# Rows of a float32r matmul stream moved to a fixed place modulo 512 bytes

## The chip, the cores and the metric

The kernel runs on one core of one Trainium2 chip. The metric is the device time of one execution in microseconds, the median of three runs: 2297.84 us before the change (2295.18 to 2297.98). Profiles are of one execution each.

## What is computed

Two transformer blocks in a row on 256 tokens with 2048 features, all in float32. Cut to what matters here:

```python
SEQ, D_MODEL, D_FF = 256, 2048, 5632

def first_block(x, ...):
    h = rms_norm(x, mix_norm_g)
    q, kv, gate_logits, conv_in = split(h @ w_in)      # NSA attention and a conformer convolution
    x = x + concatenate([attn, conv]) @ w_out
    h = rms_norm(x, ffn_norm_g)
    u = causal_depthwise_conv(h @ w_up, cw, cb)        # 2048 x 11264
    a, gate = split(u)
    x = x + (silu(gate) * a) @ w_down                  # 5632 x 2048
    return rms_norm(x, final_norm_g)

def second_block(x, c, positions, ...):
    shift_m, scale_m, gate_m, shift_f, scale_f, gate_f = split(silu(c) @ w_ada + b_ada)
    h = rms_norm_2(x, g_pre_mix) * (1.0 + scale_m) + shift_m
    z = h @ w_in                                       # into MLA attention and gated linear attention
    o = concatenate([o_mla, o_gla]) @ w_out
    x = x + gate_m * rms_norm_2(o, g_post_mix)
    h = rms_norm_2(x, g_pre_ffn) * (1.0 + scale_f) + shift_f
    f = (silu(h @ w_ffn_gate) * (h @ w_ffn_up)) @ w_ffn_down
    return x + gate_f * rms_norm_2(f, g_post_ffn)
```

## The kernel before

Activations live on the chip transposed: features on the 128 partitions, the 256 tokens (`T`) on the free axis. A *row* in this text is one tile row of that kind, 128 partitions x 256 float32 values, which is 1024 bytes in each partition. `XT` holds the 16 rows of the residual stream, and `XH`, `XL` the rows that the products read.

All large products run as float32r matmuls on operands split in two. ACT copies a piece of weights, 128x1024, from its raw buffer to `wh` (`split_h`, line 454), DVE subtracts that from the raw values into `wl` (`split_l`, line 461), and the rows are split the same way into `XH` and `XL`. Three products are summed in PSUM: high x high, high x low and low x high. The weights come as a stream of pieces over SP's DMA queue into raw buffers (three of 2048 columns), three pieces ahead of their use (`LA = 3`).

`run_group` (line 549) walks through the groups of output columns in a fixed order: w_in of block 1 (to about 275 us of the span), w_out (`oh`/`ol` rows to 354, `ch`/`cl` rows of the convolution to 399), then the FFN in two halves of up-products (from the X rows) and down-products (from the `hh`/`hl` rows, called hid here: 399 to 656 up, 656 to 785 down, and again), then block 2: w_in, the MLA products, w_out (1423 to 1515) and the SwiGLU FFN with up- and down-products in turn to the end. There are two modes. In mode "w" a 128x128 slice of weights is loaded and a row of 256 columns moves; the groups `z0`, `z1`, `f0_0` and `f0_1`, first behind an adaptive norm, move 258 columns, of which the last two both carry the shift. In mode "x" a 128x128 slice of a row is loaded and 512 weight columns move (four groups of w_in and the down-products of block 2). PE meets the three products of each row in the order in which `run_group` issues them.

All other work (norms, both attentions, convolution, gated linear attention, the modulation from `w_ada`) is written as generators that a planner issues beside the products, when its own clock says that an engine has come to them (`Clock`, `Side`, `tick`). Each instruction is issued by one helper, so the profile puts all of them at line 303; the tiles' names tell them apart.

What the change touches:
- `setup` (745): the tiles `XT`, `XH` and `XL` (16 rows of T + 2 floats each, 1032 bytes apart), `vecs`, `kc`. They live for the whole kernel in the pool `cp`, which hands out addresses in the order of these calls.
- `block1_setup` (762): the tiles of block 1's mixers, among them `oh` and `ol` (8 rows each), the attention's output for w_out.
- `pre_u0_0` (1209) and `pre_f0_0` (1828): `hh` and `hl_`, 22 rows in block 1 and 16 in block 2, the hidden rows of the FFN.
- `pre_z0` (1361): `qn` and `kn`, one tile per head, whose place `mla_gen` (1606) takes over for the MLA's output rows (`oh0`..., `ol0`...).
- `xsrc` (604), `feed_shift` (647), `ev_shift` (1470) and `ev_f` (1896): which rows a product reads, how the shift is written behind the rows, and how it is read back from PSUM, into `sh`.

Of the kernel before, what the change touches and what calls it, by code (L numbers as in the profile page):

```python
"""Two transformer blocks (NSA attention + conformer conv + conv-GLU FFN, then MLA + GLA + SwiGLU
FFN with adaptive norms) on one core.

Activations live on the chip transposed: features on the partitions, the 256 tokens on the free
axis.  Weight products run as float32r matmuls: every float32 operand is split on the chip into two
float32r parts (hi + lo, 24 mantissa bits together) and hi*hi + hi*lo + lo*hi are accumulated.
"""
# [28 lines left out]
# ----------------------------------------------------------------------------- weight stream  # L36
# [4 lines left out]
def make_plan():  # L41
    """Groups of column tiles, in the order in which the tensor engine meets them."""
# [106 lines left out]
AHEAD = 2  # L149
GROUPS, MCS, TILES, WLEN = make_plan()  # L150
# [26 lines left out]
# ----------------------------------------------------------------------------- small arrays  # L177
# [103 lines left out]
# ----------------------------------------------------------------------------- the kernel  # L281
def rev(a, n):
    """a[:, n - 1 :: -1]."""
    return bass.AP(tensor=a.tensor, offset=a.offset + n - 1, ap=[list(a.ap[0]), [-1, n]])


def halves(i, n):
    """The first piece of weights is split in two steps."""
    return ((0, n // 2), (n // 2, n)) if i == 0 else ((0, n),)


class Engine:
    """Issues on an engine, and tells the clock what was issued."""
# [13 lines left out]
class Clock:  # L307
    """About when each engine comes to the end of what it was given (in us).  Work is issued in segments: a segment
    starts when its inputs are there, and the next segment of the same work when this one has ended."""
# [29 lines left out]
    def run(self, f, dep):  # L339
        """Issues a segment; its value, its end and whether it issued anything."""  # L340
        old = self.dep, self.ends, self.n
        self.dep, self.ends, self.n = dep, {}, 0
        v = f()
        end = max(self.ends.values(), default=dep) + (self.LAT if self.n else 0)
        n = self.n
        self.dep, self.ends, self.n = old
        return v, end, n


class Flags:  # L350
    """What has been issued, from the time on at which it will be done."""
# [11 lines left out]
class Side:  # L363
    """Work that runs beside the products of the weights: a generator that yields after each segment (or, with a number,
    is left alone for that many us; "dve": until DVE has little left to do)."""
# [5 lines left out]
class Kern:  # L371
# [16 lines left out]
    # ---- helpers  # L388
# [12 lines left out]
    def bank(self):  # L401
        """A PSUM bank; free() gives it back once its last reader has been emitted."""
# [8 lines left out]
    def need(self, n):  # L411
        """Waits until n banks can be had without holding up the products of the weights."""
# [31 lines left out]
    # ---- weight stream  # L444
# [28 lines left out]
    def next_mc(self, i):  # L473
        """High parts LA pieces ahead, low parts one piece less."""
# [10 lines left out]
    def tick(self):  # L485
        """Issues what is due beside the products by the time that the tensor engine gets here."""
# [20 lines left out]
    def idle(self):  # L507
        """The tensor engine has to wait: on to the next time at which something is ready."""
# [16 lines left out]
    def later(self, f, norm):  # L525
        """As soon as the products are done (and, where f needs it, the norm's factor is there)."""
# [22 lines left out]
    def run_group(self, g):  # L549
# [20 lines left out]
        for mi in g["mcs"]:  # L570
# [8 lines left out]
            for u in range(nt if g["mode"] == "w" else 2):  # L579
                o = ps[u][:min(n, 128), :N] if g["mode"] == "w" else ps[u][:, :n]  # L580
                for q, k in enumerate(m["ks"]):
# [7 lines left out]
                    for i, (a, b) in enumerate(p):  # L589
                        self.mm(o, a, b, k == 0 and i == 0, k == kl and i == 2)  # L590
# [13 lines left out]
    def xsrc(self, k, N=T):  # L604
        return self.XH[:, k, :N], self.XL[:, k, :N]

    def ready(self, key, k):
        """Row k of what the group reads has been emitted."""
# [10 lines left out]
    # ---- norms  # L619
    # The first groups after a norm run on rows without the norm's per-token factor, which their  # L620
    # evacuation applies; meanwhile the rows are rewritten with the factor for the groups after them.
# [25 lines left out]
    def feed_shift(self, b):  # L647
        """Two more columns that carry the shift."""
        bb = b[:, :, None].to_broadcast([128, 16, 2])
        self.act(self.XH[:, :, T:], bb, AF.Copy)  # L650
        self.tt(self.XL[:, :, T:], bb, self.XH[:, :, T:].bitcast(F32), OP.subtract)
# [42 lines left out]
    def warm(self):  # L694
        """Loads the table of the square root before it is waited for."""
        self.act(self.kc[:, 3:4], self.eps, AF.Sqrt)

# [3 lines left out]
    def sums(self, parts):  # L701
        """Sum over the partitions (and over parts), in every partition."""
# [10 lines left out]
    # ---- program  # L713
# [31 lines left out]
    def setup(self):  # L745
        a = self.a
        self.XT = self.cp.tile([128, 16, T], F32, name="XT")
        self.XH = self.cp.tile([128, 16, T + 2], F32R, name="XH")
        self.XL = self.cp.tile([128, 16, T + 2], F32R, name="XL")
        self.vecs = self.cp.tile([128, VEC.n], F32, name="vecs")  # L750
        self.kc = self.cp.tile([128, 4], F32, name="kc")
        self.v.memset(self.kc[:, 0:1], EPS)
# [8 lines left out]
    # ======================================================================= block 1, mixers  # L761
    def block1_setup(self):
        tc, a, ph = self.tc, self.a, self.ph
        self.p1 = ph.enter_context(ExitStack())
        P = self.b1 = self.p1.enter_context(tc.tile_pool(name="b1", bufs=1))
        self.cat = P.tile([128, CA.n], F32, name="cat")
        self.sy.dma_start(self.cat[:, :16], a["ca"][:, :16])
        self.cacc = [P.tile([128, 4, T], F32, name=f"cacc{b}") for b in range(2)]
# [8 lines left out]
        self.oh = P.tile([128, 8, T], F32R, name="oh")  # L777
        self.ol = P.tile([128, 8, T], F32R, name="ol")
# [20 lines left out]
        # keeps the tensor engine's clock up until the first rows are there  # L799
# [120 lines left out]
    def bias_gen(self):  # L920
# [23 lines left out]
        # block n of the second 128 tokens is as far away as block n - 8 of the first; from block 7 on none is complete  # L944
# [13 lines left out]
    def cmp_gen(self):  # L958
        yield
        for kv in range(2):  # L960
            self.sy.dma_start(self.w1.rearrange("p l f -> p (l f)"), self.a["w1"][kv])
            # the even places of a block in the lower half of the partitions, the odd ones in the upper half
# [86 lines left out]
    def stat_sq(self, js, src=None, scale=None, acc="ss"):  # L1049
        """Running sum of squares over tiles of XT."""  # L1050
# [45 lines left out]
    def att_gen(self, n):  # L1096
        """Head u of pair p; its keys lie in half u of the partitions."""
# [53 lines left out]
        # columns of PT: per branch [keys 0:128 x all tokens | keys 128:256 x tokens 128:256], then cmp  # L1151
# [22 lines left out]
        # the two heads side by side, in halves of the array's columns  # L1174
# [25 lines left out]
    # ======================================================================= block 1, FFN  # L1200
# [8 lines left out]
    def pre_u0_0(self):  # L1209
# [8 lines left out]
        self.hh = P.tile([128, 22, T], F32R, name="hh")  # L1218
        self.hl_ = P.tile([128, 22, T], F32R, name="hl")
# [5 lines left out]
        self.adaT = self.cp.tile([128, 96], F32, name="adaT")  # L1225
        self.cs = self.cp.tile([128, 16], F32, name="cs")
# [3 lines left out]
    def ada_gen(self, c0, c1, P, nk, bufs, every):  # L1230
        """Column groups c0 to c1 of the modulation, nk rows of tiles at a time, one such piece every so many us."""
# [10 lines left out]
        for cg in range(c0, c1):  # L1242
# [13 lines left out]
            # sums over the partitions side by side in the array's columns, then back on to the partitions  # L1256
# [757 lines left out]
```

## Time and profile before

| | before |
|---|---|
| median of three runs | 2297.84 us (2295.18 to 2297.98) |
| span of the profiled execution | 2296.4 us |
| busy PE / weight loads | 2267.4 us (99%) / 2165.5 us (94%) |
| busy DVE / ACT / POOL | 1700.1 us (74%) / 1187.9 us (52%) / 4.9 us (0%) |
| DMA | 499.22 MB, mean 217 GB/s |

The span runs from the first to the last instruction of one profiled execution on the slowest core. Busy times add up an engine's instructions; PE and its weight loads (PEld) overlap. Matmuls are pipelined, so the duration of one is longer than the distance between the starts of two, and a busy PE need not be PE at its peak.

### The profile page before, as it was taken

The numbers are of one execution on the slowest core, as the hardware profiler recorded it, in microseconds if no ns is written. First come the engines' busy times: TensorE is split into PE (matmuls) and PEld (weight loads), VectorE is DVE, ScalarE is ACT, GpSimd is POOL, SyncE is SP. The second block draws the span as 40 slices with busy tenths as digits, with TensorE's granted clock in tenths as the row PEclk, the third lists the DMA queues.
The fourth block names the chain that finished last, engine by engine and source line by source line (L and its number), as shares of the span: only waits on it lengthen the run. The fifth ranks groups of instructions, "written<-read, shape, count | busy, mean of one in ns | idle before, by whom it ended". The sixth has DMA issues, their size and how long they took to land.

```text
span 2296.4 us, 42341 instructions
## 1 busy us (share of the span) xinstructions
PE 2267.4 (99%) x17486; PEld 2165.5 (94%) x17486; DVE 1700.1 (74%) x2631; ACT 1187.9 (52%) x1826; POOL 4.9 (0%) x16
## 2 busy tenths in 40 slices
PE   8999999999999999999999999999999999999997
PEld 8998889999999999999999889989997999889986
DVE  6998888898887788888879866577666565444455
ACT  5447786655553355555556664455444444344443
POOL 0000000000000000000000000000000000000000
PEclk9999999999999999999999999999999999999999
DMA  6544325688878787877756643546666665555553
GB/s 236 181 168 156 124 80 196 230 297 290 302 280 298 283 290 286 294 276 281 256 200 221 229 139 138 196 145 207 240 235 235 244 235 189 192 182 171 184 183 129
DMA packets 89089, 499.22 MB, mean 217 GB/s; under 512 B 9904, under 2 KB 12352, under 8 KB 42432
## 3 DMA queue, kind: packets, MB, share of 16 engines
q1 hardware_dynamic: 88896, 496.51, 61.5%
q8 instruction: 137, 2.24, 0.4%
q14 instruction: 56, 0.46, 0.1%
HBM read 494.35 MB, written 2.12 MB: 216 GB/s over the span
## 4 chain that ended last, share of the span: by engine, by line
PE 93%; DVE 4%; ACT 2%; issue 1%; DMA 1%; SPq 0%; DVEq 0%; ACTq 0%
PE ps L303 93%; DVE wl L303 1%; DMA raw<-in_wst_dram 1%; DVE cacc L303 0%; ACT wh L303 0%; DVE og L303 0%; ACT P L303 0%; ACT XH L303 0%; ACT L303 0%; DVE XL L303 0%; DVE ss L303 0%; DVE blk L303 0%; ACT vt L303 0%; ACT y L303 0%; DVE XT L303 0%
## 5 line engine op out<-in xcount | busy, mean ns | idle before, releaser
L303 ACT ACTIVATE wh<-raw 128x1024 fp32r<-128x1024 f32 (+2 forms) x741 | 781.7, 1057 | 910.7 <-PE ps L303 767.6
L303 DVE TENSOR_TENSOR wl<-raw,wh 128x1024 fp32r<-128x1024 f32 (+2 forms) x741 | 899.1, 1217 | 476.5 <-PE ps L303 410.9
L303 PE MATMUL ps<-XH,wh 128*128 128x256 f32 (+1 forms) x3840 | 1096.9, 286 | 2.6 <-ACT XH L303 2.6
L303 PE MATMUL ps<-XH,wl 128*128 128x256 f32 (+1 forms) x3840 | 1085.9, 283 | 3.9 <-DVE wl L303 3.9
L303 PE MATMUL ps<-XL,wh 128*128 128x256 f32 (+1 forms) x3840 | 1083.4, 282 | 0.1
L303 PEld LDWEIGHTS ps<-XH,wh 128*128 128x128 f32 x3840 | 726.1, 189 | 10.3 <-issue 5.8
L303 PEld LDWEIGHTS ps<-XH,wl 128*128 128x128 f32 x3840 | 727.9, 190 | 4.9 <-DVE wl L303 4.9
L303 PEld LDWEIGHTS ps<-XL,wh 128*128 128x128 f32 x3840 | 729.1, 190 | 1.0 <-DVE XL L303 0.6
L303 DVE SCALAR_TENSOR_TENSOR ac<-wa,cs,ac 128x512 f32<-128x512 f32 x360 | 269.7, 749 | 6.4
L303 PE MATMUL ps<-hh,wh 128*128 128x256 f32 x704 | 200.3, 285 | 0.0
L303 PE MATMUL ps<-hh,wl 128*128 128x256 f32 x704 | 199.2, 283 | 0.0
L303 PE MATMUL ps<-hl,wh 128*128 128x256 f32 x704 | 199.2, 283 | 0.0
L303 PE MATMUL ps<-wh,hh 128*128 128x512 f32 x352 | 139.0, 395 | 0.0
L303 PE MATMUL ps<-wl,hh 128*128 128x512 f32 x352 | 138.8, 394 | 0.0
L303 PE MATMUL ps<-wh,hl 128*128 128x512 f32 x352 | 138.8, 394 | 0.0
L303 PEld LDWEIGHTS ps<-hh,wh 128*128 128x128 f32 x704 | 135.0, 192 | 1.2 <-issue 1.2
L303 PEld LDWEIGHTS ps<-hl,wh 128*128 128x128 f32 x704 | 135.1, 192 | 0.0
L303 PEld LDWEIGHTS ps<-hh,wl 128*128 128x128 f32 x704 | 135.1, 192 | 0.0
L303 DVE SCALAR_TENSOR_TENSOR cacc<-upad,cat,cacc 128x256 f32<-128x256 f32 x240 | 99.8, 480 | 0.3 <-ACT cacc L303 0.2
L303 PEld LDWEIGHTS ps<-wh,hh 128*128 128x128 f32 x352 | 65.9, 187 | 16.4 <-issue 0.2
L303 PEld LDWEIGHTS ps<-wl,hh 128*128 128x128 f32 x352 | 65.9, 187 | 16.3
L303 PEld LDWEIGHTS ps<-wh,hl 128*128 128x128 f32 x352 | 65.9, 187 | 15.9
(321 smaller groups left out, 2113.3 us busy)
## 6 DMA issues: line engine op xcount, KB each, us to landing
raw<-in_wst_dram SPq DMA_DIRECT2D x363, 1024.0 KB, 4.9
wa<-in_wada_dram SPq DMA_DIRECT2D x176, 512.0 KB, 6.0
wa<-in_wada_dram SPq DMA_DIRECT2D x32, 256.0 KB, 5.3
raw<-in_wst_dram SPq DMA_DIRECT2D x4, 768.0 KB, 4.3
raw<-in_wst_dram SPq DMA_DIRECT2D x4, 512.0 KB, 5.6
B<-dtab SPq DMA_DIRECT2D x8, 256.0 KB, 5.1
out_dram<-og SPq DMA_DIRECT2D x8, 256.0 KB, 2.7
XT<-in_x_dram SPq DMA_DIRECT2D x3, 512.0 KB, 6.9
```

Source lines behind the costliest of these rows:

```text
L303: return f(*x, **k)
```

## The change

All rows that the tensor engine reads are put 16 bytes past the weight pieces' place modulo 512 bytes, and the strides between them become whole multiples of 512 bytes.

- A new helper `rows` makes one tile for several sets of rows. It skips `PHASE = 4` floats (16 bytes) at its start. `XH`/`XL`, `oh`/`ol` of block 1 and `hh`/`hl_` in both blocks come from it. `qn`/`kn` get the same four floats in front of each tile.
- Rows of `XH` are 384 floats apart (`XROW`, 1536 bytes), those of `XL` 256 floats (1024 bytes). `XL` has no shift columns any more: `feed_shift` puts the high part of the shift into column 256 of `XH` and the low part into column 257, and `shift` adds the two sums that come out in PSUM.
- The product with `XL` in the groups with shift has 256 columns instead of 258.
- Tiles that are no multiple of 512 bytes are moved so that the places come out: `adaT`, `gf`, `cs` and `gs` are allocated in `setup`, `oh`/`ol` and `cacc` at the head of block 1's pool, `gg` becomes 128 floats wide.
- The scratch memory for DMA descriptors is set to 1024 bytes.

The diff, without the comments that it drops:

```diff
+PHASE = 4
+XROW = 384
...
@@ run_group
-                o = ps[u][:min(n, 128), :N] if g["mode"] == "w" else ps[u][:, :n]
+                o = ps[u][:min(n, 128)] if g["mode"] == "w" else ps[u][:, :n]
...
-                        self.mm(o, a, b, k == 0 and i == 0, k == kl and i == 2)
+                        self.mm(o[:, :b.shape[1]], a, b, k == 0 and i == 0, k == kl and i == 2)
...
     def xsrc(self, k, N=T):
-        return self.XH[:, k, :N], self.XL[:, k, :N]
+        return self.XH[:, k, :N], self.XL[:, k]
...
     def feed_shift(self, b):
-        bb = b[:, :, None].to_broadcast([128, 16, 2])
-        self.act(self.XH[:, :, T:], bb, AF.Copy)
-        self.tt(self.XL[:, :, T:], bb, self.XH[:, :, T:].bitcast(F32), OP.subtract)
+        bb = b[:, :, None]
+        h = self.XH[:, :, T:T + 1]
+        self.act(h, bb, AF.Copy)
+        self.tt(self.XH[:, :, T + 1:T + 2], bb, h.bitcast(F32), OP.subtract)
+
+    def shift(self, out, p, s=1):
+        self.v.tensor_reduce(out, p[:, T:T + 2], axis=AX, op=OP.add)
+        if s != 1:
+            self.v.tensor_scalar(out, out, s, None, op0=OP.mult)
...
+    def rows(self, pool, name, parts, skip=PHASE):
+        t = pool.tile([128, skip + sum(n * w for n, w in parts)], F32R, name=name)
+        out, o = [], skip
+        for n, w in parts:
+            out.append(t[:, o:o + n * w].rearrange("p (k t) -> p k t", t=w))
+            o += n * w
+        return out
...
@@ setup
-        self.XH = self.cp.tile([128, 16, T + 2], F32R, name="XH")
-        self.XL = self.cp.tile([128, 16, T + 2], F32R, name="XL")
+        self.adaT = self.cp.tile([128, 96], F32, name="adaT")
+        self.gf = self.cp.tile([128, 16], F32, name="gf")
+        self.XH, self.XL = self.rows(self.cp, "X", ((16, XROW), (16, T)))
         self.vecs = self.cp.tile([128, VEC.n], F32, name="vecs")
         self.kc = self.cp.tile([128, 4], F32, name="kc")
+        self.cs = self.cp.tile([128, 16], F32, name="cs")
+        self.gs = self.cp.tile([128, 16], F32, name="gs")
@@ block1_setup
+        self.oh, self.ol = self.rows(P, "o", ((8, T), (8, T)))
+        self.cacc = [P.tile([128, 4, T], F32, name=f"cacc{b}") for b in range(2)]
         self.cat = P.tile([128, CA.n], F32, name="cat")
         self.sy.dma_start(self.cat[:, :16], a["ca"][:, :16])
-        self.cacc = [P.tile([128, 4, T], F32, name=f"cacc{b}") for b in range(2)]
...
-        self.oh = P.tile([128, 8, T], F32R, name="oh")
-        self.ol = P.tile([128, 8, T], F32R, name="ol")
@@ pre_u0_0 (and pre_f0_0, with 16 rows)
-        self.hh = P.tile([128, 22, T], F32R, name="hh")
-        self.hl_ = P.tile([128, 22, T], F32R, name="hl")
+        self.hh, self.hl_ = self.rows(P, "hid", ((22, T), (22, T)))
@@ pre_z0
-        self.gg = Po.tile([128, 16], F32, name="gg")
-        self.qn = [Po.tile([128, T], F32, name=f"qn{h}") for h in range(8)]
-        self.kn = [Po.tile([128, T], F32, name=f"kn{h}") for h in range(8)]
+        self.qn, self.kn = ([Po.tile([128, T + PHASE], F32, name=f"{n}{h}")[:, PHASE:] for h in range(8)] for n in ("qn", "kn"))
+        self.gg = Po.tile([128, 128], F32, name="gg")[:, :16]
@@ ev_shift
-            self.v.tensor_scalar(sh[:, e:e + 1], p[:, T:T + 1], s, None, op0=OP.mult)
+            self.shift(sh[:, e:e + 1], p, s)
@@ mla_gen
-        oh = self.omh[h] = self.b2o.tile([128, T], F32R, name=f"oh{h}", tag=f"qn{h}")
-        ol = self.oml[h] = self.b2o.tile([128, T], F32R, name=f"ol{h}", tag=f"kn{h}")
+        oh, ol = (self.b2o.tile([128, T + PHASE], F32R, name=f"{n}{h}", tag=f"{t}{h}")[:, PHASE:]
+                  for n, t in (("oh", "qn"), ("ol", "kn")))
+        self.omh[h], self.oml[h] = oh, ol
@@ ev_f
-                self.v.tensor_copy(sh[:, e:e + 1], ps[e][:, T:T + 1])
+                self.shift(sh[:, e:e + 1], ps[e])
@@ the program
-    nc = _bacc.Bacc("TRN2", target_bir_lowering=False, num_devices=1)
+    nc = _bacc.Bacc("TRN2", target_bir_lowering=False, num_devices=1, dynamic_dma_scratch_size=1024)
```

## Rows read from the trace of the kernel before

**Rows 1.** The cores' view: span and mean granted TensorE clock.
```profile
core 0: 2296.4 us, clock 0.995
```
**Rows 2.** The page: busy time (share, instructions); the chain that ended last, by engine.
```profile
PE 2267.4 (99%) x17486; PEld 2165.5 (94%) x17486; DVE 1700.1 (74%) x2631; ACT 1187.9 (52%) x1826; POOL 4.9 (0%) x16
...
PE 93%; DVE 4%; ACT 2%; issue 1%; DMA 1%; SPq 0%; DVEq 0%; ACTq 0%
```
**Rows 3.** The waits: who waited for whom, us in total, times, longest.
```profile
PE ps L303 <- DVE wl L303: 4.8, 5, 2.9
```
**Rows 4.** Timeline of PE (start, duration): X rows, 402 products from first to second.
```profile
1599.99 0.28 PE L303 MATMUL ps<-XH,wl 128*128 128x256 f32 x1
...
1648.01 0.28 PE L303 MATMUL ps<-XH,wl 128*128 128x256 f32 x1
```
**Rows 5.** Timeline of PE: hid rows of block 1, 99 products apart.
```profile
700.09 0.28 PE L303 MATMUL ps<-hh,wl 128*128 128x256 f32 x1
...
711.97 0.28 PE L303 MATMUL ps<-hh,wl 128*128 128x256 f32 x1
```
**Rows 6.** Timeline of PE: `oh` rows of block 1; five, then 120 products apart.
```profile
275.53 0.28 PE L303 MATMUL ps<-oh,wh 128*128 128x256 f32 x1
...
276.12 0.28 PE L303 MATMUL ps<-oh,wl 128*128 128x256 f32 x1
...
334.01 0.28 PE L303 MATMUL ps<-ol,wh 128*128 128x256 f32 x1
...
347.62 0.28 PE L303 MATMUL ps<-ol,wh 128*128 128x256 f32 x1
```
**Rows 7.** Timeline of PE: `oh` rows of block 2, 96 products to the second.
```profile
1469.10 0.28 PE L303 MATMUL ps<-oh,wh 128*128 128x256 f32 x1
...
1480.41 0.28 PE L303 MATMUL ps<-XH,wh 128*128 128x256 f32 x1
```
**Rows 8.** Timeline of PE: 512 weight columns moving, hid rows loaded, 99 products apart.
```profile
1970.08 0.39 PE L303 MATMUL ps<-wh,hl 128*128 128x512 f32 x1
...
1993.18 0.39 PE L303 MATMUL ps<-wh,hl 128*128 128x512 f32 x1
```
**Rows 9.** Window (columns as in rows 12; PEclk 0.50), then its timeline, four products apart.
```profile
332.30:333.80 1.50, 1.50 (x8) 1.41 (x7) 0.00 (x0) 0.89 (x1) 0.00 (x0) 0.50 0.00 0
...
332.84 0.41 PE L303 MATMUL ps<-ol,wh 128*128 128x256 f32 x1
...
333.69 0.36 PE L303 MATMUL ps<-oh,wl 128*128 128x256 f32 x1
```
**Rows 10.** Timeline of PE around the product of row 6 of `XL` (first line).
```profile
1626.39 0.28 PE L303 MATMUL ps<-XL,wh 128*128 128x256 f32 x1
1626.50 0.28 PE L303 MATMUL ps<-XH,wl 128*128 128x256 f32 x1
1626.62 0.28 PE L303 MATMUL ps<-XH,wh 128*128 128x256 f32 x1
```
**Rows 11.** Groups of instructions: count, busy us, mean ns, idle before (last line: by form).
```profile
L303 PE MATMUL ps<-XH,wh 128*128 128x256 f32 (+1 forms) x3840 | 1096.9, 286 | 2.6 <-ACT XH L303 2.6
L303 PE MATMUL ps<-hh,wh 128*128 128x256 f32 x704 | 200.3, 285 | 0.0
L303 PE MATMUL ps<-wh,hh 128*128 128x512 f32 x352 | 139.0, 395 | 0.0
...
L303 PE MATMUL ps<-wh,XH 128*128 128x512 f32 x96 | 39.6, 413 | 0.0
```
**Rows 12.** Windows: us, busy (instructions) of PE, PEld, DVE, ACT, POOL, PEclk, DMA, GB/s.
```profile
100.00:200.00 100.00, 99.45 (x821) 94.70 (x819) 91.31 (x220) 55.21 (x112) 0.57 (x2) 1.00 0.46 160
399.00:656.00 257.00, 256.38 (x2160) 254.25 (x2159) 227.78 (x326) 144.05 (x213) 0.15 (x2) 1.00 0.78 278
700.10:712.00 11.90, 11.90 (x102) 11.90 (x100) 8.09 (x9) 4.63 (x5) 0.00 (x0) 1.00 0.84 306
```
**Rows 13.** The tile `sh`: ns min/median/max of one, first and last start.
```profile
L303 DVE TENSOR_SCALAR sh<-ps x8: 148/154/159, 1196.5 to 1223.9; 128x1 f32<-128x1 f32 x8
```

More of the change, by code (lines that the diff above doesn't have):

```diff
@@ L1224, in pre_u0_0 @@
             self.gp.memset(t[:, :, 0:2], 0.0)
-        self.adaT = self.cp.tile([128, 96], F32, name="adaT")
-        self.cs = self.cp.tile([128, 16], F32, name="cs")
         self.act(self.cs, self.vec("c", 0, 16), AF.Silu)
@@ L1327, in ev_d @@
             if js[0] == 0:
-                self.gs = self.cp.tile([128, 16], F32, name="gs")
                 self.stt(self.gs, self.adaT[:, 16:32], 1.0, self.vec("g_pre", 0, 16), OP.add, OP.mult)
@@ L1828, in pre_f0_0 @@
     def pre_f0_0(self):
-        self.gf = self.cp.tile([128, 16], F32, name="gf")
         self.stt(self.gf, self.adaT[:, 64:80], 1.0, self.vec("g_pref", 0, 16), OP.add, OP.mult)
@@ L1842, in pre_f0_0 @@
         P = self.f2 = self.ph.enter_context(self.tc.tile_pool(name="f2", bufs=1))
-        self.hh = P.tile([128, 16, T], F32R, name="hh")
-        self.hl_ = P.tile([128, 16, T], F32R, name="hl")
+        self.hh, self.hl_ = self.rows(P, "hid", ((16, T), (16, T)))
         self.f = self.og.rearrange("p (u a) t -> p u (a t)", u=2)
```

## The prediction

> **What bounds the kernel now.** I read the views in this order. First the cores' view: one core, 2296.4 us, mean granted clock 0.995, nearly always the upper level of 2.4 GHz [rows 1]. Then the page's busy shares and the chain of work that ended last: PE is busy 99% of the span and carries 93% of the chain, while DVE and ACT have slack [rows 2]. Then the waits of PE: the longest sum is 4.8 us, so almost no time goes on waiting for anybody [rows 3]. What is left is the pace at which TensorE starts one product after the other. The mean durations in the groups cannot show that pace, because products overlap (283 ns each, started some 119 ns apart). So I went to the timeline and divided the distance between two starts by the number of products between them.
>
> The products of the X rows start every 48.02 us / 402 = 119.4 ns [rows 4]. Those of the hid rows (`hh`, `hl`) start every 11.88 / 99 = 120.0 ns [rows 5]. The products of the `oh` rows do the same work, 128x256 with a 128x128 weight load beside it, and start every 13.61 / 120 = 113.4 ns in block 1 [rows 6] and every 11.31 / 96 = 117.8 ns in block 2 [rows 7]. With 512 columns the gap is 23.10 / 99 = 233.3 ns [rows 8]. In one stretch the granted clock was 0.50 (1.2 GHz), after PE had waited: there the gap is 0.85 / 4 = 212 ns [rows 9]. Half of it, 106 ns, is what 256 columns would take at 2.4 GHz if they streamed without a stall. So 7 to 14 ns are lost in every product at the full clock, and the loss differs between operands that differ in nothing I can see but their place.
>
> The places are known from the built program, modulo 512 bytes. Every weight piece begins at 288, and so does every 128-column slice of it. The hid rows of block 1 begin at 288, +0 from the weights. `oh`/`ol` of block 1 begin at 224 (-64), those of block 2 at 352 (+64). Rows of 258 floats are 1032 bytes apart, so XH runs over -160 to -40 and XL over -32 to +88 in steps of 8. So +0 goes with 120.0, +64 with 117.8 and -64 with 113.4. No whole stretch has +16. It occurs once per pass, in XL's row 6: there the product's gap is 0.11 us, and that of the product after it 0.12 [rows 10].
>
> **The change part by part.** *Places.* I added up the tiles in the order in which the pools hand them out (each rounded up to 32 bytes). The weight pieces then begin 150 x 512 bytes behind the X tile, so every row of XH (1536 apart) and XL (1024 apart) lies at +16; so do hid in both blocks and `oh`/`ol` of block 1. Not all rows do: `ch` comes to +0 and `cl` to +32, the MLA rows, 1056 bytes apart, run through +16, +48, +80 and so on, and `cqs`/`ckh` keep other places. These are some 960 of 16,300 products; I cost them at nothing.
>
> The unknown is the pace at +16. Bounds from rows: 106 ns below (no stall left), and above it the 120.0 of +0 plus one more such step as lies between 113.4 and 120.0, so 126.6. I take 113.4, the best pace that any stretch holds, because the one row at +16 is among the quick ones and stands in a stream that is slow otherwise. That reason is thin: this row's gap depends on its neighbours too. Counts: 3 x 3840 = 11,520 products of X rows, 3 x 704 = 2112 of hid, 3 x (352 + 96) = 1344 with 512 columns [rows 11].
> X: 11,520 x (119.4 - 113.4) = 69.1 us.
> hid: 2112 x (120.0 - 113.4) = 13.9 us.
> 512 columns: weights are the moving operand, the row the loaded one, and the distance becomes -16. The bounds are 0 and one step of 6.6 ns, 8.9 us; I take half, 4.4 us.
> `oh` of block 1: at 113.4 to 117.8 already; 256 x 3 products hold both blocks, the gain is under 1 us, taken as 0.
> Together 87.4 us, all on the chain, as PE is the chain.
>
> *What is late next.* DVE, with the products 5% quicker: it is busy 227.78 of 257 us in the first half of block 1's up-products and 91.31 of 100 us from 100 us on [rows 12]. At 257 x 113.4 / 119.4 = 244 us it would be at 93%, with some 16 of its 29 idle us left. So I let the FFN keep its gain. From 100 to 200 us DVE would come to 96%, and norms and attention hang on it in turn. I give half of the gain there back: some 1560 X products x 6.0 / 2 = 4.7 us. DMA would go from 278 to 293 GB/s in the same up-products; 306 stand in a hid stretch already [rows 12], so 0.
>
> *Small edits.* The shift now travels as two columns of XH (high and low part) and none of XL; each product has 256 or 258 columns as before, and the one of XL loses two. Sixteen additions of two columns take the place of sixteen one-column operations, of which eight take 154 ns each in the median [rows 13], and one scaling is added: 0.2 us on DVE, off the chain. `adaT`, `gf`, `cs`, `gs` are only allocated earlier. The scratch for DMA descriptors shrinks from 16 KB to 1 KB, which pays for the longer rows; all transfers here leave on SP's queue. If the smaller one did matter, weights would come late; PE's longest wait for a weight piece is 2.9 us now [rows 3], which stands for one such event. I take 0. No wait is added and no step moved.
>
> *Sum.* 87.4 - 4.7 = 82.7 us off the profiled 2296.4. The median of the three runs, 2297.84, lies 1.4 us above the span, so I forecast 2297.8 - 82.7 = 2215 us.
>
> A rule of the Trainium skill speaks against all this. What the rows show: equal products at 113.4, 117.8 and 120.0 ns [rows 5 to 7]. "TensorE: Matmul & The Clock Gate" (Step-by-step: what each phase is for) says that PE has two independent SBUF read ports, and that loading the next tile's weights does not steal read bandwidth from the running matmul; "SBUF — State Buffer" (Who interferes with whom) adds that PE never waits on anyone. By that rule the place would be without effect and the time stay at 2298; the trace does not fit it, as the loss changes with the operand, but it does not name the place as the cause.
>
> **The rivals.**
> *A weaker pace.* The same -64 rows also ran at 117.8 before they fell into 113.4 (the first five gaps of block 1's `oh` products are 0.59 us [rows 6]), so one place has more than one steady pace and the slow one may win. Then X gains 11,520 x 1.6 = 18.4, hid 2112 x 2.2 = 4.6, 512 columns nothing: 2275 us. Up to 116 ns it would be 2250.
> *No stall left.* If +16 keeps the two streams from ever meeting, the gap lies between 106 and 113.4, say 110: X 108.3, hid 21.1, 512 columns 1344 x 13.3 / 2 = 8.9, less 10 for DVE before 275 us: 2170 us. Against it: no stretch shows it, and the fastest gap seen at +16 is 0.11.
> *Slower.* All rows now share one place, so a bad meeting of row read and weight load is no longer averaged over 16 places but repeats in every product. hid shows that this happens: 120.0 without any scatter at +0, only 16 bytes away. It decides from 119.5 ns on. At 120.0 X costs 11,520 x 0.6 = 6.9 us more: 2305. At the upper bound of 126.6 it is 11,520 x 7.2 + 2112 x 6.6 = 97 more: 2395.
> *No effect.* The spread comes from something else than place (stage, DMA traffic, other engines' reads): 2298. Against it: hid holds 120.0 evenly with DMA at 306 GB/s and DVE busy 8.09 of 11.9 us [rows 12], `oh` goes from 118 to 113.4 within one stage [rows 6], and no row that I read ties a pace to a load.
>
> **How the numbers follow.** Forecast 0.46, with 2200 to 2235 as its own range; weaker pace 0.16; no stall 0.15; slower 0.16; no effect 0.07. Faster by over 0.2% (some 4.6 us, about what a measurement of this kernel can tell from no change) comes to 0.77, within it 0.08 with a sliver of the slower case, slower 0.15. The range must take in the weaker pace and no effect, and most of the stall-free case: 2155 to 2300 leaves out the slower case and the low end, together under 2 in 10.
>
> **What would show it.** In the profile after, the distance of starts in the X and hid stretches decides everything: 113 to 114 confirms, 117 to 118 is the weaker pace, under 112 the stall-free one, 120 or more the slower one. X and hid must come to the same pace, since they have the same place; if they differ, place modulo 512 is not the whole cause. `ch`/`cl`, `cqs` and the MLA rows must not gain. If the pace is reached but the time is not, PE's waits for DVE before 275 us must have grown. The forecast is wrong if the one quick row at +16 owed its gap to its neighbours.

## The result and the profile after

The changed kernel takes 2261.48 us (median of four runs, 2257.57 to 2265.83), the kernel before 2297.14 (four runs): a ratio of 0.985, interval 0.983 to 0.986. So 36 us were gained where 83 were forecast. The direction was right, and the range of 2155 to 2300 us, drawn wide enough for several rivals, held the time; of the forecast gain 43% arrived. The runs of the changed kernel lie 8.3 us apart, those of before 2.8 us; that spread, as the experiments show, is part of the answer.

Apart from the span, the views of [rows 1 to 3] have hardly moved. Cores' view, busy times and chain from the page, and PE's longest sum of waits, all of the changed kernel:

```profile
core 0: 2263.9 us, clock 0.996
...
PE 2234.7 (99%) x17486; PEld 2137.7 (94%) x17486; DVE 1698.5 (75%) x2632; ACT 1187.7 (52%) x1826; POOL 4.9 (0%) x16
...
PE 93%; DVE 4%; ACT 2%; issue 1%; DMA 1%; SPq 0%; DVEq 0%; ACTq 0%
...
PE ps L305 <- DVE wl L305: 4.1, 3, 3.2
```

PE still carries 93% of the chain and waits no longer than before; nothing new became late. So the answer lies again in the distance between the starts of products. The high and low rows are now one tile (`X`, `hid`), and the timeline puts two products of the same names into one line (x2). The lines with `wl` stand alone, one for each three products, so I count by those. Timeline of PE in the changed kernel (start, duration): X rows with 252 such lines from the first to the second, X rows with 49, hid rows with 113.

```profile
1560.06 0.28 PE L305 MATMUL ps<-X,wl 128*128 128x256 f32 x1
...
1649.77 0.28 PE L305 MATMUL ps<-X,wl 128*128 128x256 f32 x1
...
1007.19 0.28 PE L305 MATMUL ps<-X,wl 128*128 128x256 f32 x1
...
1023.85 0.28 PE L305 MATMUL ps<-X,wl 128*128 128x256 f32 x1
...
1043.28 0.28 PE L305 MATMUL ps<-hid,wl 128*128 128x256 f32 x1
...
1082.83 0.28 PE L305 MATMUL ps<-hid,wl 128*128 128x256 f32 x1
```

89.71 us / (3 x 252) = 118.7 ns; 16.66 / (3 x 49) = 113.3; 39.55 / (3 x 113) = 116.7. The forecast asked for one pace at one place. For products of 256 columns the long stretches of this trace have three, each kept to the hundredth of a microsecond for tens of microseconds: in the stretch at 113.3 every distance between two `wl` lines is 0.34 us, at 116.7 every one is 0.35, at 118.7 each is 0.35 or 0.36. Before the change hid held 120.0 and the scattered X rows 119.4 [rows 4, 5].

Does the load of the other engines choose the pace? Windows of the same trace (columns as in [rows 12]): the stretch at 113.3, then 116.7, then 118.7.

```profile
1007.00:1040.00 33.00, 33.00 (x294) 33.00 (x293) 30.58 (x43) 17.90 (x24) 0.00 (x0) 1.00 0.79 290
1043.00:1100.00 57.00, 57.00 (x494) 56.67 (x494) 48.58 (x72) 28.92 (x42) 0.00 (x0) 1.00 0.78 280
1560.00:1650.00 90.00, 90.00 (x760) 90.00 (x760) 58.16 (x63) 38.25 (x44) 0.00 (x0) 1.00 0.68 244
```

The quickest stretch has DVE at 93% and DMA at 290 GB/s, the slowest DVE at 65% and 244 GB/s. More load does not go with a slower pace.

What happens where the pace changes? Timeline of PE about 1005 us, where 116.7 turns into 113.3; in brackets the idle time before a product and what ended it:

```profile
1004.21 0.28 PE L305 MATMUL ps<-X,wl 128*128 128x256 f32 x1
1004.41 0.43 PE L305 MATMUL ps<-ac,vecs 128*32 128x128 f32 x8
1004.77 0.51 PE L305 MATMUL ps<-X,wh 128*128 128x256 f32 x2
...
1006.10 0.33 PE L305 MATMUL ps<-vecs,ac 128*128 128x128 f32 x1 [0.35 <-ACT ac L305]
1006.19 0.48 PE L305 MATMUL ps<-X,wh 128*128 128x256 f32 x2
```

The modulation's sums (`ac`) and their transposition break into the stream, and the stream starts anew. No stretch of more than 60 products without a break changes its pace on the way in this trace. That gave the theory to be tested: **at one place the stream can keep several steady paces, and each restart lets it fall into one of them.** Rivals: the pace follows the load after all (the same work beside it gives the same pace), or the place alone gives one pace and the mixture comes from something else that is fixed in the program.

### The profile page after: what moved, and what is told of

Read it like the earlier page. It is cut to its first block, busy times and chain, and to the rows that moved or that the text cites. A ratio compares the mean times of both kernels' runs of the same rounds, so it can differ in the third digit from the quotient of the medians.

```text
span 2263.9 us, 42338 instructions
## 1 busy us (share of the span) xinstructions
PE 2234.7 (99%) x17486; PEld 2137.7 (94%) x17486; DVE 1698.5 (75%) x2632; ACT 1187.7 (52%) x1826; POOL 4.9 (0%) x16
## 4 chain that ended last, share of the span: by engine, by line
PE 93%; DVE 4%; ACT 2%; issue 1%; DMA 1%; SPq 0%; DVEq 0%; ACTq 0%
PE ps L305 93%; DVE wl L305 1%; DMA raw<-in_wst_dram 1%; DVE cacc L305 0%; ACT wh L305 0%; DVE og L305 0%; ACT P L305 0%; DVE X L305 0%; ACT X L305 0%; ACT L305 0%; DVE ss L305 0%; DVE blk L305 0%; ACT y L305 0%; ACT vt L305 0%; DVE XT L305 0%
## 5 line engine op out<-in xcount | busy, mean ns | idle before, releaser
L305 PE MATMUL ps<-X,wh 128*128 128x256 f32 (+1 forms) x7680 | 1374.8, 281 | 3.6 <-ACT X L305 2.9
L305 ACT ACTIVATE wh<-raw 128x1024 fp32r<-128x1024 f32 (+2 forms) x741 | 781.5, 1056 | 875.6 <-PE ps L305 798.8
L305 PEld LDWEIGHTS ps<-X,wh 128*128 128x128 f32 x7680 | 1174.5, 188 | 12.3 <-issue 5.8
L305 PE MATMUL ps<-X,wl 128*128 128x256 f32 (+1 forms) x3840 | 1073.8, 280 | 3.4 <-DVE wl L305 3.4
L305 PEld LDWEIGHTS ps<-X,wl 128*128 128x128 f32 x3840 | 721.3, 188 | 4.0 <-DVE wl L305 4.0
L305 PE MATMUL ps<-hid,wh 128*128 128x256 f32 x1408 | 247.8, 279 | 0.0
L305 PE MATMUL ps<-wh,hid 128*128 128x512 f32 x704 | 220.1, 394 | 0.0
L305 PEld LDWEIGHTS ps<-hid,wh 128*128 128x128 f32 x1408 | 214.1, 188 | 1.2 <-issue 1.2
L305 PE MATMUL ps<-hid,wl 128*128 128x256 f32 x704 | 196.0, 278 | 0.0
L305 PE MATMUL ps<-wl,hid 128*128 128x512 f32 x352 | 138.1, 392 | 0.0
L305 PEld LDWEIGHTS ps<-hid,wl 128*128 128x128 f32 x704 | 132.2, 188 | 0.0
```

What stands on the lines that cost most here:

```text
L305: return f(*x, **k)
```

## The experiments

**The same program again.** No edit.

> The changed kernel once more, unaltered; what is read is the pace of starts in each stretch of its trace, against the first trace of the same program (118.7 ns at 400 to 475 us, 116.7 at 480 to 1003, 113.3 at 1007 to 1040, 118.7 at 1560 to 1650). Theory of the steady paces: at one place the stream can run at one of several paces, 113.3, 116.7 and 118.7 ns, and falls into one of them at each restart; then the same three paces come back, but not always in the same stretches, and the time lies in 2255 to 2268 us. Rival, load: the pace follows what DVE, ACT and DMA do at that time; their work is the same in both executions, so each stretch has the pace that it had in the first trace. Rival, place alone: one pace for the place, and the other two come from something else that is fixed in the program; again each stretch as before.

It took 2256.96 us (one run). Timeline of PE in this execution (50 lines of `wl` from first to second), and the window of this stretch. It is the stretch that ran at 113.3 in the first trace: it begins behind the same transposition, which here comes after a wait of 0.34 us for ACT, there after 0.35.

```profile
1000.08 0.28 PE L305 MATMUL ps<-X,wl 128*128 128x256 f32 x1
...
1017.88 0.28 PE L305 MATMUL ps<-X,wl 128*128 128x256 f32 x1
...
1000.00:1035.00 35.00, 35.00 (x298) 35.00 (x297) 31.67 (x44) 17.98 (x24) 0.00 (x0) 1.00 0.77 285
```

17.80 / (3 x 50) = 118.7 ns in place of 113.3, with DVE at 90% (93% there) and DMA at 285 GB/s (290). Elsewhere it went the other way: hid from 740 to 769 us ran at 113.3 here and at 116.7 in the first trace. The same program with the same load has other paces in the same stretches. Averaged over each trace the X products stand 117.6 ns apart in the first and 116.9 here, those of hid 116.5 and 115.4 (breaks left out); 11,520 x 0.7 + 2112 x 1.1 = 10.4 us, which is enough for the 8.9 us between the two spans (2263.9 and 2255.0). Load and place alone both fall for this pair, unless two chips differ: whether both executions were on one chip is not known. The streams further down settle that within one execution.

**Streams alone.** A kernel of 192 streams of 96 products, three passes over 64 places of the rows; this is its inner part:

```python
for r in range(4):
    for k in range(8):
        c = slice(128 * k, 128 * k + 128)
        xh = R[:, p + k * T:p + k * T + T]
        xl = R[:, p + (8 + k) * T:p + (8 + k) * T + T]
        for a, b in ((wh[:, c], xh), (wh[:, c], xl), (wl[:, c], xh)):
            nc.tensor.matmul(o[:, :T], a, b, start=m == 0, stop=m == last)
```

> This kernel leaves out everything of the blocks: it has 3 x 64 streams of 96 products 128x256 float32r each (the same triples of high and low parts), on one tile of weights and one of rows, without DMA and with almost nothing on DVE and ACT. In the 64 streams of a pass the rows begin 0, 8, 16, ... 504 bytes past the weights' place modulo 512. First pass: each stream follows the one before without a break; second: four small float32 products stand between two streams; third: each stream starts after a wait for ACT. Theory of the steady paces: paces depend on the place even without any other load: 120.0 ns at +0; one of 113.3, 116.7 and 118.7 at +16; 113.3 or 117.8 at -64; and at some places the pace differs between the passes, since they start differently. Rival, load: with nothing beside it every place runs at one pace, between 106 and 113 ns. Rival, place alone: a pace for each place, the same in all three passes.

Timeline of PE, one line for each stream (start, duration of all its 96 products): in the second pass the rows at +0, +16, +64 and +112, then the same places in the third pass.

```profile
747.30 11.78 PE L66 MATMUL ps<-R,W 128*128 128x256 f32 x96
...
771.44 11.47 PE L66 MATMUL ps<-R,W 128*128 128x256 f32 x96
...
842.94 11.15 PE L66 MATMUL ps<-R,W 128*128 128x256 f32 x96
...
914.86 11.20 PE L66 MATMUL ps<-R,W 128*128 128x256 f32 x96
...
1514.07 11.75 PE L66 MATMUL ps<-R,W 128*128 128x256 f32 x96
...
1539.37 11.45 PE L66 MATMUL ps<-R,W 128*128 128x256 f32 x96
...
1614.44 11.55 PE L66 MATMUL ps<-R,W 128*128 128x256 f32 x96
...
1690.33 11.18 PE L66 MATMUL ps<-R,W 128*128 128x256 f32 x96
```

At +64 the same 96 products took 11.15 us after one kind of start and 11.55 after the other; the other three places kept theirs. The whole duration holds a slower start, so I also took the mean distance between the starts of single products in the second half of each stream, in ns (good to about 0.1):

| place | no break | behind small products | behind a wait |
|---|---|---|---|
| +0 | 120.0 | 120.0 | 120.0 |
| +16 | 116.7 | 116.7 | 116.7 |
| +32 | 116.7 | 117.8 | 117.8 |
| +64 | 113.3 | 113.3 | 117.8 |
| +80 | 118.3 | 119.9 | 120.1 |
| +112 | 113.3 | 113.3 | 113.3 |
| +144 | 118.7 | 116.7 | 118.7 |
| +192 | 113.3 | 117.8 | 117.8 |

The places 8 bytes off these multiples of 16 lay between 118.3 (+56) and 122.2 ns (+120), and each place agreed with the one 256 bytes further on to 0.2 ns in all three passes. Without any load beside it the pace depends on the place: the load theory falls a second time, and 106 to 113 ns were seen at no place. The streams also take eight PSUM buffers in turn, but places 64 bytes apart share one, and +0 and +64 differ. At +16 the start made no difference here, as the rival expected; that was left for a later kernel.

**The rows at +0 and at -64.** Only the place in the tiles that `rows` makes is changed: `ROWPLACE` is 0 for +0 and 112 floats for -64, and `PAD` (4 and 132) keeps the other tiles in their places modulo 512.

```diff
-        t = pool.tile([128, skip + sum(n * w for n, w in parts)], F32R, name=name)
-        out, o = [], skip
+        t = pool.tile([128, PAD + sum(n * w for n, w in parts)], F32R, name=name)
+        out, o = [], ROWPLACE
```

> The changed kernel with its rows (X, hid, o of block 1) at +0 instead of +16 bytes; everything else lies where it lay. Theory of the steady paces: at +0 the pace is the 120.0 ns that hid held there before the change, with no better one to fall into: 11,520 X products x (120.0 - 119.4) = 7 us over the kernel before, 2300 to 2306 us. Rival, load or strides: what counts is that the rows don't scatter; then +0 does what +16 does, 2258 to 2268 us.

> The changed kernel with its rows (X, hid, o of block 1) at -64 bytes (+448) from the weights' place, where o of block 1 held 113.4 and began at 118 ns before the change. Theory of the steady paces: a mixture of 113.4 and 117.8 ns, with few other paces: between 2297 - 11,520 x 1.6 - 2112 x 2.2 = 2274 us and 2297 - 11,520 x 6.0 - 2112 x 6.6 = 2214 us. Rival, place alone with 113.4 as the pace of -64: 2214 us. Rival, load: as at +16, 2258 to 2268 us.

At +0 the kernel took 2293.87 us, at -64 2230.22, with the kernel before at 2297.02 on the same chip (one run of each). Timeline of PE at +0: X rows (277 lines of `wl` apart), then 512 columns (73 apart).

```profile
1574.21 0.28 PE L307 MATMUL ps<-X,wl 128*128 128x256 f32 x1
...
1673.93 0.28 PE L307 MATMUL ps<-X,wl 128*128 128x256 f32 x1
...
1970.05 0.39 PE L307 MATMUL ps<-wl,hid 128*128 128x512 f32 x1
...
2019.69 0.39 PE L307 MATMUL ps<-wl,hid 128*128 128x512 f32 x1
```

99.72 / 831 = 120.0 ns in the X rows, as hid had before, and no other pace in any long stretch of X or hid. So it is not the strides that help: equal strides at +0 make the X products slower than the scattered ones were. The time came out 6 us below the bound of my expectation because of the 512 columns, which I had left out: 49.64 / 219 = 226.7 ns in place of 233.3 [rows 8], and 1344 x 6.6 = 8.9 us. Timeline of PE at -64, two stretches of X rows, 288 and 84 lines of `wl` apart:

```profile
1530.03 0.28 PE L307 MATMUL ps<-X,wl 128*128 128x256 f32 x1
...
1627.95 0.28 PE L307 MATMUL ps<-X,wl 128*128 128x256 f32 x1
...
1750.01 0.28 PE L307 MATMUL ps<-X,wl 128*128 128x256 f32 x1
...
1779.69 0.28 PE L307 MATMUL ps<-X,wl 128*128 128x256 f32 x1
```

97.92 / 864 = 113.3 and 29.68 / 252 = 117.8 ns: the paces of [rows 6] and [rows 7], mixed, and a time between the two bounds. The 512 columns kept 228.9 ns here in every long stretch.

**The rows at +112**, the place with one pace in all passes (`ROWPLACE = 28`, `PAD = 132`).

> The changed kernel with its rows (X, hid, o of block 1) at +112 instead of +16 bytes. Alone, the streams at +112 and +368 were the only ones that ran at 113.3 ns in all three passes. Theory of the steady paces: at +112 there is one pace to fall into, so the X and hid products hold 113.3 to 113.4 ns through nearly all stretches, whatever interrupts them: 11,520 x 6.0 + 2112 x 6.6 = 83 us less than before, less some us that DVE takes back before 275 us, with 512 columns between 226.7 (9 us less) and 233.3 (0): 2200 to 2222 us. Rival, neighbours: alone there is no DMA, DVE and ACT beside the stream; if these disturb it, other paces come back and the time stays near the 2230 us of the rows at -64, or above.

2224.56 us (2222.79 to 2227.06), ratio to before 0.969 (0.967 to 0.970): 2.6 us above what I expected. PE's longest waits, then its timeline: X rows, 293 lines of `wl` apart, hid rows, 93 apart, and 512 columns, 49 apart.

```profile
PE ps L307 <- DVE wl L307: 5.7, 7, 2.5
...
1525.29 0.28 PE L307 MATMUL ps<-X,wl 128*128 128x256 f32 x1
...
1624.91 0.28 PE L307 MATMUL ps<-X,wl 128*128 128x256 f32 x1
...
694.15 0.28 PE L307 MATMUL ps<-hid,wl 128*128 128x256 f32 x1
...
725.77 0.28 PE L307 MATMUL ps<-hid,wl 128*128 128x256 f32 x1
...
1935.12 0.39 PE L307 MATMUL ps<-wl,hid 128*128 128x512 f32 x1
...
1969.42 0.39 PE L307 MATMUL ps<-wl,hid 128*128 128x512 f32 x1
```

X 99.62 / 879 = 113.3 ns, hid 31.62 / 279 = 113.3, and every long stretch of either in this trace comes to that pace, whatever broke into it. So load does not disturb it: the rival falls. A break has its price even so. Behind the one at 472.8 us, and alike behind others, the stream first takes 13 products of 116 to 123 ns, 118.8 in the mean, before it holds 113.3. With such beginnings and the short stretches the X products stand 114.1 ns apart over the whole trace, and 71 us arrived of the 83 that one pace throughout would give. The 512 columns stay at 34.30 / 147 = 233.3.

**The places put back, the rest left changed.** `rows` takes the place and the padding as its last two arguments here.

```diff
-        self.XH, self.XL = self.rows(self.cp, "X", ((16, XROW), (16, T)))
+        self.XH, self.XL = self.rows(self.cp, "X", ((16, T + 2), (16, T + 2)), 88, 88 + 108)
...
-        self.oh, self.ol = self.rows(P, "o", ((8, T), (8, T)))
+        self.oh, self.ol = self.rows(P, "o", ((8, T), (8, T)), 112, 132)
...
-        self.hh, self.hl_ = self.rows(P, "hid", ((22, T), (22, T)))
+        self.hh, self.hl_ = self.rows(P, "hid", ((22, T), (22, T)), 0, 4)
...
-        self.hh, self.hl_ = self.rows(P, "hid", ((16, T), (16, T)))
+        self.hh, self.hl_ = self.rows(P, "hid", ((16, T), (16, T)), 0, 4)
```

> The changed kernel with X, hid and o of block 1 put back where they were before the change, relative to the weights (X rows 1032 bytes apart from -160 and -32 on, hid at +0, o at -64); the shift in two columns of XH, the MLA rows, the other moved tiles and the small descriptor scratch stay as changed. Theory (the places carry the whole gain): 2294 to 2299 us, as before the change. Rival, small edits: if two columns less, the other tiles' places or the scratch gave or took anything, the time moves off 2297 by that much; a third of the measured gain would be 2285 us.

2290.95 us against 2295.94, ratio 0.998 (0.997 to 0.999): below the expected 2294 to 2299. My edit was not quite a return: it put hid of block 2 at +0 too, which the built program before had at +64. The timeline shows it; 512 columns, 87 lines of `wl` apart:

```profile
1960.43 0.39 PE L305 MATMUL ps<-wl,hid 128*128 128x512 f32 x1
...
2019.59 0.39 PE L305 MATMUL ps<-wl,hid 128*128 128x512 f32 x1
```

59.16 / 261 = 226.7 ns; 1056 products x 6.6 = 7.0 us. Without them the kernel would stand at 2298, 2 us over before, and the interval of the ratio is as wide as that. So the small edits give nothing that can be told from zero.

**Starts, 512 columns, and both operands moved.** A second kernel of streams alone; a small product of 8, 16, ... 128 columns stands ahead of each of 16 streams at +16, +112 and -64.

```python
if cols:
    nc.tensor.matmul(e[:, :cols], f, g[:, :cols], start=True, stop=True)
```

> Again streams of float32r products alone, without the blocks. First, 32 places 8 bytes apart with the 128x128 slice of a row loaded and 512 weight columns moving, once back to back, once behind a wait for ACT. Then 256 columns moving at places 4, 12, 20, ... bytes. Then 16 streams each at +16, +112 and -64, started behind one small float32 product of 8, 16, ... 128 columns, so that each stream starts at another distance from the one before. Then rows at +112 from the weights while both are moved together by 32, 64, ... bytes. Theory of the steady paces: the start decides among the paces that a place allows, so +16 shows two or three of 113.3, 116.7, 118.7, -64 two (113.3, 117.8) and +112 one (113.3) over the 16 starts; moving both changes nothing; 512 columns at +0 run at 226.7, at the mirror of +16 at 226.7 and 233.3. Rival, start has no say and something else in the full kernel makes the mixture: each place shows one pace over its 16 starts (116.7 at +16, as in all three passes alone).

Timeline of PE, one line for each stream (72 products): four at +16, two at +112, two at -64, each behind a small product of another width.

```profile
1041.62 8.79 PE L68 MATMUL ps<-R,W 128*128 128x256 f32 x72
...
1050.39 8.66 PE L68 MATMUL ps<-R,W 128*128 128x256 f32 x72
...
1059.03 8.41 PE L68 MATMUL ps<-R,W 128*128 128x256 f32 x72
...
1067.41 8.80 PE L68 MATMUL ps<-R,W 128*128 128x256 f32 x72
...
1181.45 8.46 PE L68 MATMUL ps<-R,W 128*128 128x256 f32 x72
...
1189.89 8.42 PE L68 MATMUL ps<-R,W 128*128 128x256 f32 x72
...
1325.00 8.73 PE L68 MATMUL ps<-R,W 128*128 128x256 f32 x72
...
1333.70 8.43 PE L68 MATMUL ps<-R,W 128*128 128x256 f32 x72
```

By the distances between their products the first three are the paces of the changed kernel, 118.7, 116.7 and 113.3 ns, at one place; what differs by design is the width of one small product ahead of them. Over all 16 starts +16 fell into 118.7 fourteen times and once into each other; -64 into 117.8 twice and 113.3 fourteen times; +112 into 113.3 sixteen times. So with no other work, in one execution, one place has several paces and the start decides among them. The PSUM buffer, which also changes from stream to stream, does not: the second and third start at +16 had the same buffers as the tenth and eleventh, which ran at 118.7. All but the usual pace came behind the three narrowest products: from 32 columns on every start at one place ended alike. Rows at +112 with both operands moved by 32, 64, ... 480 bytes ran at 113.3 in all 16 streams: only the distance counts. Places 4 bytes off a multiple of 8 ran at 116.9 to 123.4. With 512 columns, +0 ran at 226.7, +120 too, +112 at 233.3; for +16 I expected a mixture of 226.7 and 233.3, and alone it kept 233.3. The mixture did stand in the changed kernel: in both of its traces the last stretch of 512 columns ran at 226.7 ns (from 2176 us in the first), the long ones before it at 233.3 to 233.4.

**A place for each kind of product.** The kernel with rows at +112, and hid of block 2, which is only ever the loaded operand beside 512 columns, at +0:

```diff
-        self.hh, self.hl_ = self.rows(P, "hid", ((16, T), (16, T)))
+        self.hh, self.hl_ = self.rows(P, "hid", ((16, T), (16, T)), 0)
```

> The kernel with rows at +112, but hid of block 2, whose slices are only ever the loaded operand beside 512 moving columns, at +0: alone and in the kernel with all rows at +0 these products ran at 226.7 ns, at +112 they run at 233.3 to 233.4. Theory (pace by place, for each kind of product its own): 352 x 3 x (233.4 - 226.7) = 7 us less than 2224.6: 2214 to 2221 us, and hid's 512-column stretches at 226.7 to 226.9 ns. Rival: the 512-column products gain but the stream then waits for DVE or the weights, as the gain lies where pieces are needed fastest: 2222 to 2228 us.

2217.41 us (2215.44 to 2217.45), ratio 0.965 (0.964 to 0.967): faster than both kernels, and 7.2 us below the one with all at +112. Its 512 columns in the timeline, 51 lines of `wl` apart, at 34.68 / 153 = 226.7 ns:

```profile
1930.25 0.39 PE L307 MATMUL ps<-wl,hid 128*128 128x512 f32 x1
...
1964.93 0.39 PE L307 MATMUL ps<-wl,hid 128*128 128x512 f32 x1
```

## Where the prediction was right and where it failed

*What bounds the kernel* was right: PE's distance between starts, and nothing that waits. The place of the rows relative to the weights sets it, as the prediction had taken from three stretches. The rival "no effect" falls with `place0`, `place448` and `place112`: three kernels that differ in the place of the rows and the padding behind it lie at 2293.87, 2230.22 and 2224.56 us.

*The step that failed* is the pace at +16, "I take 113.4": the X products came to 117.6 ns in the mean, and to no one pace. Its reason was one row in a stream whose rows lie at 32 places: row 6 of `XL` had a gap of 0.11 us [rows 10]. The prediction itself called that thin, since a gap depends on its neighbours, and so it was: a stream that is all +16 has three paces, and 113.3 is one that it falls into seldom (once in 16 starts alone; a stretch of 34 us and a few short ones in the profiled execution). Averaged over the trace, the X products stand 117.6 ns apart, hid's 116.5, those with 512 columns 231.4 (before: 119.4, 119.9 and 233.1, in this order; distances between starts, breaks left out). The terms of the sum become X 11,520 x 1.8 = 20.7 us for 69.1, hid 2112 x 3.4 = 7.2 for 13.9, 512 columns 1344 x 1.7 = 2.3 for 4.4: 30 us for 87, beside 32.5 between the two profiled spans.

*The rival that came true* is the weaker pace, given 0.16. It named the right mechanism, more than one steady pace at one place, and its 2250 to 2275 us hold the measured time. But it came to it by luck: the five gaps that it read as a steady 117.8 [rows 6] lie between 114 and 123 ns, and after two more products of these rows other work breaks in: that is no steady pace. That -64 also has a steady pace of 117.8 was shown only by `place448`.

*The slower rival* looked for a bad meeting in every product. It exists, at +0, 16 bytes away: 120.0 ns throughout in `place0`. Its price there was about right for X (11,520 x 0.6 = 7 us), but at the same place the 512 columns have the quickest pace seen of them, 226.7, worth 8.9 us, which the rival had left out: the kernel at +0 came out no slower than before.

*DVE before 275 us.* The 4.7 us given back were not seen. The first product of the `oh` rows starts at 275.53 before [rows 6] and at 270.41 after: 5.1 us arrived, more than the X products before it gave by their pace (119.2 to 117.4 ns, 1560 x 1.8 = 2.8 us). With rows at +112 it starts at 270.43 in `place112` and at 267.88 in `split_places`, whose instructions and places are the same up to there: 5.1 and 7.7 us of 1560 x (119.2 - 114.2) = 7.8. What the rest of that stretch takes thus differs by 2.6 us between two executions, and in one of them nearly all arrived. PE's longest sum of waits for DVE is 4.8 us before, 4.1 after, 5.7 and 4.7 in these two; no run shows DVE taking half. In the FFN the gain was kept: block 1's first up-half, from its first X product to the first of hid, took 257.1 us before, 252.9 after and 245.2 at +112, and 2112 x (119.4 - 113.5) = 12.5 us is what the pace gives for these 11.9.

*X and hid at one pace* was the test that the prediction set itself. They share the three paces, not a common mean. So "place modulo 512 is not the whole cause", as it said; what the runs add to it is the start. The other test held: the products of `ch`/`cl`, `cqs` and the MLA rows went from 117.8, 118.3 and 117.8 ns in the mean to 117.0, 118.0 and 117.5. The `oh`/`ol` rows of block 1, put at no gain, lost some: from 114.8 to 118.2 ns, 1.3 us in 384 products.

*Small edits* were worth nothing that can be told from zero, as forecast (`old_places`). The new sum over two columns takes no longer than the operation it replaced (154 ns in the median [rows 13]): 150 ns, 16 times.

The rule of the Trainium skill that spoke against the change does not hold here. Streams with no other work beside them, of products alike but for the place, kept paces from 113.3 to above 120 ns (`micro1`). The Trainium skill, "TensorE: Matmul & The Clock Gate" (Step-by-step: what each phase is for), says that loading the next weights does not steal read bandwidth from the running matmul. By that these streams would be equal; the measurement decides. That the two reads meet somewhere would fit a pace that depends only on their distance, but no run shows it.

What stays open: why a place has just the paces that it has, and why a start ends in one or the other. That the start decides was shown by starts that differ; which moment of it counts was not tried, and whether a start of the same kind ends alike in another execution was not either.

## What to carry to other kernels

When TensorE is the bound and waits for nobody, divide the distance of starts by the products between them, stretch by stretch; a mean duration of overlapped products hides a loss of several per cent. Where the pace differs between equal products, measure it in a stream of these products alone, over all places of one operand against the other and with several kinds of start, and choose the place whose worst pace is good, not the one whose best is: here +112 instead of +16 was worth 37 us more. Choose it for each kind of product by itself, since here the best place for 256 moving rows is not the best for 512 moving weight columns.

## What the runs showed of the hardware

- A float32r stream with weight loads beside it settles into one steady pace until something breaks into it: in the kernels 113.3, 116.7, 117.8, 118.7 or 120.0 ns for 256 columns and 226.7, 228.9 or 233.3 for 512. Alone, over all places, others were seen up to 123.4 (`micro1`, `micro2`). At 2.4 GHz (granted clock 1.00) 113.3 ns are 272 cycles, 120.0 are 288, 226.7 are 544 and 233.3 are 560: the columns plus 16, 32, 32 and 48.
- The same program takes other paces in the same stretches in two executions, and its span moves with them: 2263.9 and 2255.0 us at +16. Five runs at +16 spread over 8.9 us; four each of `place112` and `split_places`, where the long stretches of each kind have one pace, over 4.3 and 2.0.
- The pace repeats when the distance between the rows' and the weights' places grows by 256 bytes (`micro1`), and stays when both move together (`micro2`, tried at +112). Distances of 4 bytes off a multiple of 8 gave 116.9 to 123.4 ns.
